# A decoder layer on one core: one more pair by seven products in five groups, and the memory mixed block by block

## The chip, the cores and the metric

The kernel runs on one core of a Trainium2 chip. Its time is the time of one execution on the device in microseconds (us), as a median of several runs. The engines named below are TensorE (PE in the rows; it multiplies matrices, and its weight loads are PEld), VectorE (DVE), ScalarE (ACT), GpSimd (POOL) and SyncE (SP, which issues nearly all DMAs). Matrix products accumulate in PSUM banks of 128 x 512 numbers; everything else lies in SBUF.

## What is computed

One layer of a decoder for 256 tokens of width 2048, in f32: a token mixer (mLSTM heads and dilated attention heads behind one input projection), cross-attention into 256 memory tokens, and a SwiGLU channel mixer, each with a residual and a layer norm. Cut to what carries the weights:

```python
def reference(x, mem, w_in, gate_b, conv_w, conv_b, mh_g, rel_bias, w_out, xq, xk, xv, xo,
              w1, w3, w2, ln_g, ln_b):
    for l in range(DEPTH):
        proj = x @ w_in[l]
        q_m, k_m, v_m, o_m, i_m, f_m, q_a, k_a, v_a = split_columns(proj, IN_SPLITS)
        y_m = mlstm_mixer(q_m, k_m, v_m, o_m, i_m, f_m, conv_w[l], conv_b[l], gate_b[l], mh_g[l])
        y_a = dilated_attention(q_a, k_a, v_a, rel_bias)
        y = jnp.concatenate([y_m, y_a], axis=-1) @ w_out[l]
        x = layer_norm(DEEPNORM_ALPHA * x + y, ln_g[l, 0], ln_b[l, 0])
        y = memory_cross_attention(x, mem, xq[l], xk[l], xv[l], xo[l])
        x = layer_norm(DEEPNORM_ALPHA * x + y, ln_g[l, 1], ln_b[l, 1])
        y = swiglu_ffn(x, w1[l], w3[l], w2[l])
        x = layer_norm(DEEPNORM_ALPHA * x + y, ln_g[l, 2], ln_b[l, 2])
    return x
```

`memory_cross_attention` computes `x @ wq`, `mem @ wk`, `mem @ wv`, a softmax over the memory tokens and `o @ wo`; `swiglu_ffn` is `(silu(x @ w1) * (x @ w3)) @ w2` with a hidden width of 5632.

## The kernel before

**Precision.** A matmul takes its operands in a reduced f32 format. So `split` (L112 to L115) writes each operand as a high part, a cast on ScalarE (L114), and a low part, the rest, by a subtraction on VectorE (L115). A product of two split operands takes three matmuls: high by high, high by low, low by high. Tokens and memory are split once (`Operand.put`); the weights, 1 MB at a time, are split as they arrive.

**Groups and pairs.** Each weight product is cut into groups of 1024 output columns. A group is the sum over 2048 input rows in eight pairs (w2, over a half of the hidden width, in twelve): a pair is two tiles of 128 input rows by 1024 columns, one DMA (L199, or L210 where two arrays are read) into one of three raw buffers (RAW). Split weights have five buffers for each part (SPLIT).

**A plain pair** takes 24 matmuls of 128x512 (two token halves, two row tiles, two column halves, three each). **A pair by seven products** treats the pair as a 2 x 2 block matrix times a 2 x 2 block matrix and uses seven block products in place of eight: 21 matmuls. For this VectorE forms sums of the weight blocks (`sums`: L292 over 1024 columns, L296 and L297 over 512), which are split as well, and the token block has to be mixed (`Operand.mix`: four differences of 128x128, L145 to L148, and a split of 512 columns). Where the unsplit token block is gone, `mix_again` first adds high and low part (L156). In `gemm_seven` a plan gives the order of pairs: a number is a plain pair, a number in brackets, as `(2,)`, is a pair by seven products. The products go to eight PSUM banks: P1, P5, P7 and Q6 belong to sevens alone; once the last seven of the plan is through, `early` (L652 to L669 or L671 to L686) combines them, and P2, P3, Q4 and E are added at the end of the group (L691 in `whole`, L650 in `add`).

**Order of the stages on TensorE**, with the names that the rows carry: input features i0 and i1, first rows v0, attention with i2 and i3, gates, i4 and i5, v1, v2, i6, i7 and the mLSTM, memory keys xk0 and xk1, output projection wo0 and wo1, xk2 and xk3, memory values xv0 and xv1, queries xq0 to xq3 with the cross-attention, its output xo0 and xo1, then the channel mixer: f0 to f10 (the first half of the hidden units), w2a0 and w2a1 (the second product's first half, one group for each half of the columns), f12 to f20, w2b0 and w2b1, and the last norm.

**Order within an engine.** Each engine takes its instructions strictly in the order of its queue. That order is fixed when the kernel is built, by a scheduler that reorders the program on a modelled timeline; so an edit in one place moves rows in others. `tc.issue_after(latest["lo"])` puts the instructions under it behind the latest low part. Small tiles come from a pool of NSLOT slots of 4 KB for each partition (`big` takes a slot, `slot` half of one); a slot is used again as soon as its last reader is through, and the next writer waits for that reader.

**Mixing.** The blocks of x are mixed ahead of v0 (`in_rows`), the blocks of the memory ahead of xv0 (VALUES = 1, 4, 6), those of the attention's output ahead of xo0. `hidden` turns the hidden units of each f group by TensorE transposes into `hT`; the blocks in SEVENS are copied out of PSUM (L1123) and mixed at once, the others only split. hT in rows is a high or low part of such a block, hTm a mixed one.

Of the kernel before, what the change touches and what calls it, by code (L numbers as in the profile page):

```python
# [11 lines left out]
F32 = mybir.dt.float32  # L12
# [7 lines left out]
P = 128  # L20
# [14 lines left out]
W = 1024  # L35
NSLOT, RAW, SPLIT = 34, 3, 5
LAG, HEAD, POOLED, LAG2 = 6, 8, 5, 8
WARM = 2

SEVENS = (2, 4, 6, 8, 13, 15, 17)  # L40

# [11 lines left out]
def decoder_layer(ctx: ExitStack, tc: tile.TileContext, A):  # L53
# [726 lines left out]
    def in_rows(i):  # L780
        rows, plan = [], [0, 1, (2,), 3, 4, (5,), 6, 7]
        if not xT.mixed:
            xT.mix_again(2)
            xT.mix_again(5)
        banks = gemm_seven(xT, fetch(A["w_v"][i], f"v{i}"), KT, f"v{i}", plan, into_rows(rows, f"v{i}r"))
        whole(rows, banks)
        return rows
# [10 lines left out]
    nc.sync.dma_start(out=gb, in_=A["gate_b"])  # L798
    gw = const.tile([P, KT, 8], F32, tag="gw", name="gw")
    nc.sync.dma_start(out=gw, in_=A["w_gate"])  # L800

    gw2 = const.tile([P, KT, 40], F32R, tag="gw2", name="gw2")
    gz = slot("gwz")
# [10 lines left out]
    es, least_norm = gates()  # L814
    free(sel_t)
    for j in range(2):
# [77 lines left out]
    vx, x1 = [[None] * 4 for _ in range(2)], Operand("x1")  # L894
    with tc.issue_after(latest["lo"]):
        for j in VALUES:
            memT.mix_again(j)

# [14 lines left out]
    one, two, three = VALUES  # L913
    values(0, [0, 2, (one,), 3, (two,), 5, (three,), 7])
    values(1, [(one,), 0, (two,), 2, (three,), 3, 5, 7], turn_in)
# [66 lines left out]
    ln = Norm(1, "l1")  # L982
    for j in (1, 3):
        oT.mix_again(j)
    plan = [0, 2, (1,), 4, (3,), 5, 6, 7]
    banks = gemm_seven(oT, fetch(A["xo"][0], "xo0"), KT, "xo0", plan, into_z(0, ALPHA))
# [147 lines left out]
    def w2_first():  # L1134
        plan = [0, 1, 3, (2,), 5, (4,), 7, (6,), 9, (8,), 10, 11]
        for c in range(2):
            banks = gemm_seven(
                hT, fetch(A["w2"][c][:half], f"w2a{c}"), 2 * half, f"w2a{c}", plan, into_z(c, ALPHA),
                last=c == 1,
            )  # L1140
            for m in range(2):
                add(m, c, banks, scale=1.0)
# [129 lines left out]
```

## Time and profile before

| | |
|---|---|
| median of 3 runs | 1541.11 us (1541.36, 1539.5, 1541.11) |
| the profiled execution's own time | 1540.81 us |
| its span, first to last instruction | 1539.0 us, so 1.8 us lie around it |
| mean granted TensorE clock | 0.998 |
| busy: VectorE, ScalarE, GpSimd | 1233.4, 797.0, 9.3 us |
| moved by DMA | 301.37 MB, 196 GB/s over the span |

In the rows below, a line of the timeline gives start, duration, engine, line of the kernel, operation and tile; in brackets stands how long the engine idled just before, and what ended that. Buffer numbers are left out there, so that `xv0l` is any low part of xv0's weights, and `xk3r` any slot that was first called so. A row with x2 or more joins instructions that follow each other on that engine. The rows of busy time in stretches give for each stretch its length, then the busy us of PE, PEld, DVE, ACT and POOL with the count of instructions, the granted clock, the busy share of the DMA engines and GB/s.

### The profile page before, as it was taken

How to read it: one execution, taken by the hardware profiler on the slowest of the kernel's cores; microseconds unless marked ns; L12 is line 12 of the kernel's file. 1: busy time of each engine (PE TensorE's matmuls, PEld its weight loads, DVE VectorE, ACT ScalarE, POOL GpSimd, SP SyncE). 2: the span in 40 equal slices, each digit the busy share in tenths (PEclk: the TensorE clock that was granted, in tenths of full speed). 3: DMA queues.
4: the chain of work that ended last, by engine and by line, in shares of the span. 5: the costliest groups of instructions: out<-in, count | busy, mean ns of one | idle time of the engine just before them, and what ended most of it. 6: DMA issues, size and time to landing. Idle time of an engine off the chain costs nothing.

```text
span 1539.0 us, 19369 instructions
## 1 busy us (share of the span) xinstructions
PE 1522.7 (99%) x7394; PEld 1273.8 (83%) x7394; DVE 1233.4 (80%) x1663; ACT 797.0 (52%) x1054; POOL 9.3 (1%) x18
## 2 busy tenths in 40 slices
PE   9999999999999999999999999999999999999997
PEld 7888888888888878888888888887788888888885
DVE  7665788787799888657798788888788878888897
ACT  5444645554544555445557454555545455455551
POOL 0000000000000000000000000000000000000000
PEclk9999999999999999999999999999999999999999
DMA  8674445664654546445564555665455666567552
GB/s 303 208 272 165 140 172 210 232 237 160 232 191 172 205 171 221 162 165 179 177 218 165 174 182 192 218 195 200 156 215 208 200 192 194 192 205 260 197 186 109
DMA packets 83419, 301.37 MB, mean 196 GB/s; under 512 B 7213, under 2 KB 9466, under 8 KB 59774
## 3 DMA queue, kind: packets, MB, share of 16 engines
q1 hardware_dynamic: 83326, 300.14, 56.6%
q8 instruction: 58, 0.95, 0.2%
q14 instruction: 35, 0.29, 0.1%
HBM read 297.99 MB, written 4.21 MB: 196 GB/s over the span
## 4 chain that ended last, share of the span: by engine, by line
PE 95%; DVE 3%; DMA 1%; issue 0%; ACT 0%; DVEq 0%; SPq 0%; ACTq 0%
PE w2a1P L323 2%; PE w2a0P L323 2%; PE w2b0P L323 2%; PE w2b1P L323 2%; PE f10P L323 2%; PE v1P L323 2%; PE xo0P L323 2%; PE wo0P L323 2%; PE f4P L323 2%; PE f14P L323 2%; PE f6P L323 2%; PE f20P L323 2%; PE f16P L323 2%; PE f18P L323 2%; PE v0P L323 2%; PE wo1P L323 2%
## 5 line engine op out<-in xcount | busy, mean ns | idle before, releaser
L114 ACT CAST w2a1h<-w2a1w 128x1024 fp32r<-128x1024 f32 (+1 forms) x24 | 22.5, 980 | 23.3 <-PE w2a1E L323 14.5
L114 ACT CAST w2a0h<-w2a0w 128x1024 fp32r<-128x1024 f32 (+1 forms) x24 | 22.8, 980 | 17.8 <-PE w2a0E L323 10.7
L115 DVE TENSOR_TENSOR w2a0l<-w2a0w,w2a0h 128x1024 fp32r<-128x1024 f32 (+1 forms) x24 | 26.5, 1129 | 6.1 <-ACT w2a0h L114 6.1
L115 DVE TENSOR_TENSOR w2a1l<-w2a1w,w2a1h 128x1024 fp32r<-128x1024 f32 (+1 forms) x24 | 26.3, 1128 | 5.6 <-ACT w2a1h L114 5.6
L114 ACT CAST w2b0h<-w2b0w 128x1024 fp32r<-128x1024 f32 (+1 forms) x20 | 19.3, 987 | 17.3 <-PE w2b0E L323 9.8
L114 ACT CAST w2b1h<-w2b1w 128x512 fp32r<-128x512 f32 (+1 forms) x28 | 19.8, 758 | 12.9 <-PE w2b0E L323 5.4
L323 PE MATMUL w2a0P<-w2a0h,hT 128*128 128x512 f32 x80 | 26.2, 391 | 0.2 <-ACT w2a0h L114 0.2
L323 PE MATMUL w2a1P<-w2a1h,hT 128*128 128x512 f32 x80 | 25.4, 389 | 0.0
L114 ACT CAST wo1h<-wo1w 128x1024 fp32r<-128x1024 f32 (+1 forms) x16 | 15.6, 1001 | 18.9 <-PE wo1E L323 11.3
L264 PE MATMUL f0b<-f0h,x 128*128 128x512 f32 x64 | 25.4, 397 | 0.0
L114 ACT CAST f12h<-f12w 128x1024 fp32r<-128x1024 f32 (+1 forms) x16 | 15.6, 1000 | 18.7 <-PE f12E L323 9.9
L265 PE MATMUL f0b<-f0l,x 128*128 128x512 f32 x64 | 25.1, 392 | 0.1
L114 ACT CAST xv0h<-xv0w 128x1024 fp32r<-128x1024 f32 (+1 forms) x16 | 15.2, 970 | 18.5 <-PE xv0E L323 7.1
L115 DVE TENSOR_TENSOR w2b0l<-w2b0w,w2b0h 128x1024 fp32r<-128x1024 f32 (+1 forms) x20 | 22.2, 1137 | 3.0 <-ACT w2b0h L114 3.0
L115 DVE TENSOR_TENSOR v0l<-v0w,v0h 128x1024 fp32r<-128x1024 f32 (+1 forms) x16 | 18.2, 1154 | 7.8 <-ACT v0h L114 7.7
L115 DVE TENSOR_TENSOR xo0l<-xo0w,xo0h 128x1024 fp32r<-128x1024 f32 (+1 forms) x16 | 18.2, 1153 | 7.3 <-ACT xo0h L114 7.2
L114 ACT CAST v0h<-v0w 128x1024 fp32r<-128x1024 f32 (+1 forms) x16 | 15.7, 1000 | 16.0 <-PE v0E L323 9.9
L114 ACT CAST v2h<-v2w 128x1024 fp32r<-128x1024 f32 (+1 forms) x16 | 15.6, 1000 | 16.2 <-PE v2E L323 10.8
L115 DVE TENSOR_TENSOR w2b1l<-w2b1w,w2b1h 128x512 fp32r<-128x512 f32 (+1 forms) x28 | 22.7, 854 | 1.5 <-ACT w2b1h L114 1.5
L387 PE MATMUL i0b<-xT,i0h 128*128 128x512 f32 x64 | 22.6, 427 | 0.8 <-ACT i0h L114 0.8
L115 DVE TENSOR_TENSOR wo0l<-wo0w,wo0h 128x1024 fp32r<-128x1024 f32 (+1 forms) x16 | 18.2, 1153 | 6.4 <-ACT wo0h L114 6.4
L387 PE MATMUL xk1b<-mT,xk1h 128*128 128x512 f32 x64 | 23.0, 401 | 0.3 <-ACT xk1h L114 0.3
(1719 smaller groups left out, 5556.6 us busy)
## 6 DMA issues: line engine op xcount, KB each, us to landing
w2a0w<-in_w SPq DMA_DIRECT2D x12, 1024.0 KB, 4.8
w2a1w<-in_w SPq DMA_DIRECT2D x12, 1024.0 KB, 5.7
w2b0w<-in_w SPq DMA_DIRECT2D x10, 1024.0 KB, 4.9
w2b1w<-in_w SPq DMA_DIRECT2D x10, 1024.0 KB, 5.0
v0w<-in_w_v SPq DMA_DIRECT2D x8, 1024.0 KB, 5.1
v1w<-in_w_v SPq DMA_DIRECT2D x8, 1024.0 KB, 4.8
v2w<-in_w_v SPq DMA_DIRECT2D x8, 1024.0 KB, 4.8
wo0w<-in_w_out SPq DMA_DIRECT2D x8, 1024.0 KB, 4.9
```

Of the source, the lines that this page charges most:

```text
L114: SC.copy(hi, src)
L115: latest["lo"] = V.tensor_tensor(out=lo, in0=src, in1=as_f32(hi), op=ALU.subtract).ins
L264: T.matmul(banks[m][c], xh, wh[:, cs], start=n == 0, stop=False)
L265: T.matmul(banks[m][c], xh, wl[:, cs], start=False, stop=False)
L323: T.matmul(of[to], lhsT, rhs, start=to not in begun, stop=end)
L387: T.matmul(banks[f], wh[:, cs], op.both(kt), start=kt == 0, stop=end, skip_group_check=True)
```

## The change

Five groups (v0, v2, xo0, w2a0, w2a1) take one more pair by seven products and one plain pair less. v1 keeps two sevens, with block 4 in place of block 5. For this, block 4 and 6 of x in place of block 5, block 5 of the attention's output and block 10 of the hidden units are mixed as well. In w2a's plan the sevens now stand at every second place from the third on. The memory's blocks are mixed one after each pair of xv0's plan (`mix_next`), no longer all three ahead of it. There is one slot more; the gates' two weight tiles move from a pool of their own into slots that are freed behind the gates.

```diff
--- before.py
+++ after.py
@@ -33,11 +33,11 @@
 NEG = -1.0e30
 U = 2 * S - 1
 W = 1024
-NSLOT, RAW, SPLIT = 34, 3, 5
+NSLOT, RAW, SPLIT = 35, 3, 5
 LAG, HEAD, POOLED, LAG2 = 6, 8, 5, 8
 WARM = 2
 
-SEVENS = (2, 4, 6, 8, 13, 15, 17)
+SEVENS = (2, 4, 6, 8, 10, 13, 15, 17)
 
 VALUES = (1, 4, 6)
 
@@ -778,10 +778,10 @@
         return features(gemm_features(xT, A["w_qk"][i], f"i{i}", load, last), f"i{i}")
 
     def in_rows(i):
-        rows, plan = [], [0, 1, (2,), 3, 4, (5,), 6, 7]
+        rows, plan = [], [0, 1, (2,), 3, (4,), 5, *([6] if i == 1 else [(6,)]), 7]
         if not xT.mixed:
-            xT.mix_again(2)
-            xT.mix_again(5)
+            for j in (2, 4, 6):
+                xT.mix_again(j)
         banks = gemm_seven(xT, fetch(A["w_v"][i], f"v{i}"), KT, f"v{i}", plan, into_rows(rows, f"v{i}r"))
         whole(rows, banks)
         return rows
@@ -796,10 +796,11 @@
     nc.sync.dma_start(out=cw, in_=A["conv"])
     gb = const.tile([8, 1], F32, tag="gb", name="gb")
     nc.sync.dma_start(out=gb, in_=A["gate_b"])
-    gw = const.tile([P, KT, 8], F32, tag="gw", name="gw")
+    gw_t, gw2_t = slot("gw"), big("gw2")
+    gw = gw_t[:, : KT * 8].rearrange("p (k c) -> p k c", k=KT)
     nc.sync.dma_start(out=gw, in_=A["w_gate"])
 
-    gw2 = const.tile([P, KT, 40], F32R, tag="gw2", name="gw2")
+    gw2 = gw2_t[:, : KT * 40].rearrange("p (k c) -> p k c", k=KT)
     gz = slot("gwz")
     V.memset(gz, 0.0)
     V.tensor_copy(gw2[:, :, 8:32], gz.rearrange("p (k c) -> p k c", k=KT)[:, :, :24])
@@ -812,7 +813,7 @@
         attention(2 * j, qk0[j], qk0[2 + j], [va[m][0] for m in range(2)], tb)
     qk1 = in_features(2) + in_features(3)
     es, least_norm = gates()
-    free(sel_t)
+    free(sel_t, gw_t, gw2_t)
     for j in range(2):
         attention(4 + 2 * j, qk1[j], qk1[2 + j], [va[m][1] for m in range(2)], tb)
     free(*va[0], *va[1])
@@ -892,9 +893,12 @@
 
 
     vx, x1 = [[None] * 4 for _ in range(2)], Operand("x1")
-    with tc.issue_after(latest["lo"]):
-        for j in VALUES:
-            memT.mix_again(j)
+    to_mix = list(VALUES)
+
+    def mix_next():
+        if to_mix:
+            with tc.issue_after(latest["lo"]):
+                memT.mix_again(to_mix.pop(0))
 
     def values(g, plan, between=None):
         rows = []
@@ -911,7 +915,7 @@
             x1.put(j, turned([z[m][j // 2] for m in range(2)], j % 2, f"x1p{j}"))
 
     one, two, three = VALUES
-    values(0, [0, 2, (one,), 3, (two,), 5, (three,), 7])
+    values(0, [0, 2, (one,), 3, (two,), 5, (three,), 7], mix_next)
     values(1, [(one,), 0, (two,), 2, (three,), 3, 5, 7], turn_in)
 
 
@@ -980,9 +984,9 @@
         cross(h)
 
     ln = Norm(1, "l1")
-    for j in (1, 3):
+    for j in (1, 3, 5):
         oT.mix_again(j)
-    plan = [0, 2, (1,), 4, (3,), 5, 6, 7]
+    plan = [0, 2, (1,), 4, (3,), 6, (5,), 7]
     banks = gemm_seven(oT, fetch(A["xo"][0], "xo0"), KT, "xo0", plan, into_z(0, ALPHA))
     for m in range(2):
         ln.add(m, 0, banks, scale=1.0)
@@ -1132,7 +1136,7 @@
     n, half = FFN // 256, 12
 
     def w2_first():
-        plan = [0, 1, 3, (2,), 5, (4,), 7, (6,), 9, (8,), 10, 11]
+        plan = [0, 1, (2,), 3, (4,), 5, (6,), 7, (8,), 9, (10,), 11]
         for c in range(2):
             banks = gemm_seven(
                 hT, fetch(A["w2"][c][:half], f"w2a{c}"), 2 * half, f"w2a{c}", plan, into_z(c, ALPHA),
```

Three places show what moves on VectorE. The first is the begin of xv0, the first half of the memory values (mT is the memory, mTr and the slot xk3r hold blocks that are being mixed, mTm a mixed block, xv0t and xv0s the sums for a seven). Before:

```order
L115 TENSOR_TENSOR kx6_4583<-xk2r1_4386,kx6_4583 128x2x256
L296 TENSOR_TENSOR xv0s1_4729<-xv0t1_4728,xv0w1_4726 128x512
L115 TENSOR_TENSOR kx7_4586<-xk3t0_4573,kx7_4586 128x2x256
L156 TENSOR_TENSOR xk3r1_4578<-mT1_3122 128x512
L156 TENSOR_TENSOR mTr1_4623<-mT4_3222 128x512
L156 TENSOR_TENSOR mTr4_4632<-mT6_3274 128x512
L297 TENSOR_TENSOR xv0s1_4729<-xv0s1_4729,xv0w1_4726 128x512
L292 TENSOR_TENSOR xv0t4_4806<-xv0w4_4804 128x1024
L145 TENSOR_TENSOR xk3r1_4578<-xk3r1_4578 128x128
L146 TENSOR_TENSOR xk3r1_4578<-xk3r1_4578 128x128
L145 TENSOR_TENSOR mTr1_4623<-mTr1_4623 128x128
L146 TENSOR_TENSOR mTr1_4623<-mTr1_4623 128x128
```

Changed:

```order
L115 TENSOR_TENSOR xv0l1_4674<-xv0w0_4655,xv0h1_4673 128x1024
L156 TENSOR_TENSOR xk3r1_4602<-mT1_3146 128x512
L145 TENSOR_TENSOR xk3r1_4602<-xk3r1_4602 128x128
L146 TENSOR_TENSOR xk3r1_4602<-xk3r1_4602 128x128
L292 TENSOR_TENSOR xv0t1_4743<-xv0w1_4741 128x1024
L147 TENSOR_TENSOR xk3r1_4602<-xk3r1_4602 128x128
L115 TENSOR_TENSOR xv0l4_4701<-xv0w2_4698,xv0h4_4700 128x1024
L296 TENSOR_TENSOR xv0s1_4744<-xv0t1_4743,xv0w1_4741 128x512
L148 TENSOR_TENSOR xk3r1_4602<-xk3r1_4602 128x128
L115 TENSOR_TENSOR xv0l5_4717<-xv0w2_4698,xv0h5_4716 128x1024
L156 TENSOR_TENSOR mTr1_4689<-mT4_3246 128x512
L403 TENSOR_TENSOR xk2r1_4410<-xk3b0_4421,xk2r1_4410 128x256
```

Before, the three additions L156 stood together behind xv0s1's first sum (L296), and the mixing of the three blocks went on interleaved. Now block 1 is mixed first, alone, among the low parts of the two plain pairs, and block 4 (read out of mT4) begins some nine rows later.

The second place is the group f10 while the hidden units of f8 are turned and mixed (f8ru becomes the mixed block hTm8; f10t2 and f10s2 are the sums for the seven of pair 2). Before:

```order
L145 TENSOR_TENSOR f8ru_8875<-f8r11_8878 128x128
L146 TENSOR_TENSOR f8ru_8875<-f8r11_8878 128x128
L147 TENSOR_TENSOR f8ru_8875<-f8r11_8878,f8ru_8875 128x128
L115 TENSOR_TENSOR hT9_8988<-f8p1_8983,hT9_8988 128x2x256
L148 TENSOR_TENSOR f8ru_8875<-f8r11_8878,f8ru_8875 128x128
L115 TENSOR_TENSOR f10l2_9095<-f10t2_9072,f10h2_9094 128x1024
L115 TENSOR_TENSOR hT8_8969<-f8r11_8878,hT8_8969 128x2x256
L115 TENSOR_TENSOR hTm8_8976<-f8ru_8875,hTm8_8976 128x512
L296 TENSOR_TENSOR f10s2_9073<-f10t2_9072,f10w2_9069 128x512
L297 TENSOR_TENSOR f10s2_9073<-f10s2_9073,f10w2_9069 128x512
L115 TENSOR_TENSOR f10l2_9105<-f10s2_9073,f10h2_9104 128x1024
```

Changed:

```order
L292 TENSOR_TENSOR f10t2_9115<-f10w2_9112 128x1024
L296 TENSOR_TENSOR f10s2_9116<-f10t2_9115,f10w2_9112 128x512
L691 TENSOR_TENSOR f8ru_8918<-f8ru_8918,f8P2_8680 128x512
L115 TENSOR_TENSOR f10l3_9097<-f10w1_9077,f10h3_9096 128x1024
L691 TENSOR_TENSOR f8r00_8919<-f8r00_8919,f8P3_8681 128x512
L297 TENSOR_TENSOR f10s2_9116<-f10s2_9116,f10w2_9112 128x512
L691 TENSOR_TENSOR f8r00_8919<-f8r00_8919,f8Q4_8682 128x512
L691 TENSOR_TENSOR f8r01_8920<-f8r01_8920,f8E_8683 128x512
```

The sums of f10s2 (L296, L297) stood behind the mixing of block 8 and its two subtractions; now they stand ahead of the mixing, among the additions that end f8.

The third place is the begin of w2a0 while the hidden units of f10 are turned (w2a0t2 and w2a0s2 are the sums for its first seven, w2a0t4 and w2a0s4 for its second). Before:

```order
L115 TENSOR_TENSOR w2a0l2_9462<-w2a0w2_9447,w2a0h2_9461 128x1024
L292 TENSOR_TENSOR w2a0t2_9449<-w2a0w2_9447 128x1024
L292 TENSOR_TENSOR w2a0t4_9527<-w2a0w4_9525 128x1024
L115 TENSOR_TENSOR hT11_9334<-f10p1_9329,hT11_9334 128x2x256
L296 TENSOR_TENSOR w2a0s2_9450<-w2a0t2_9449,w2a0w2_9447 128x512
L115 TENSOR_TENSOR w2a0l2_9472<-w2a0t2_9449,w2a0h2_9471 128x1024
L297 TENSOR_TENSOR w2a0s2_9450<-w2a0s2_9450,w2a0w2_9447 128x512
L296 TENSOR_TENSOR w2a0s4_9528<-w2a0t4_9527,w2a0w4_9525 128x512
L297 TENSOR_TENSOR w2a0s4_9528<-w2a0s4_9528,w2a0w4_9525 128x512
L115 TENSOR_TENSOR w2a0l2_9482<-w2a0s2_9450,w2a0h2_9481 128x1024
```

Changed:

```order
L292 TENSOR_TENSOR w2a0t2_9466<-w2a0w2_9464 128x1024
L145 TENSOR_TENSOR f10ru_9272<-f10r11_9275 128x128
L146 TENSOR_TENSOR f10ru_9272<-f10r11_9275 128x128
L115 TENSOR_TENSOR hT10_9366<-f10r11_9275,hT10_9366 128x2x256
L297 TENSOR_TENSOR w2a0s4_9545<-w2a0s4_9545,w2a0w4_9542 128x512
L147 TENSOR_TENSOR f10ru_9272<-f10r11_9275,f10ru_9272 128x128
L115 TENSOR_TENSOR w2a0l2_9489<-w2a0t2_9466,w2a0h2_9488 128x1024
L148 TENSOR_TENSOR f10ru_9272<-f10r11_9275,f10ru_9272 128x128
L115 TENSOR_TENSOR hTm10_9373<-f10ru_9272,hTm10_9373 128x512
L115 TENSOR_TENSOR hT11_9385<-f10p1_9380,hT11_9385 128x2x256
L296 TENSOR_TENSOR w2a0s2_9467<-w2a0t2_9466,w2a0w2_9464 128x512
L297 TENSOR_TENSOR w2a0s2_9467<-w2a0s2_9467,w2a0w2_9464 128x512
```

Before, w2a0s2's sums stood behind the two subtractions that end hT10 and hT11. Now the mixing of block 10 (L145 to L148 and hTm10) stands ahead of them too, between w2a0t2 and w2a0s2, and the seven that needs w2a0s2 comes one plain pair earlier in the plan.

## Prediction

> **What bounds the kernel now.** I read the page first: how busy each engine is, then by engine the chain that ended last.
>
> ```profile
> PE 1522.7 (99%) x7394; PEld 1273.8 (83%) x7394; DVE 1233.4 (80%) x1663; ACT 797.0 (52%) x1054; POOL 9.3 (1%) x18
> PE 95%; DVE 3%; DMA 1%; issue 0%; ACT 0%; DVEq 0%; SPq 0%; ACTq 0%
> ```
>
> TensorE is the bound: 95% of the chain is matmuls, and only some 16 us of 1539 are not covered by one. A matmul less is time less, unless TensorE then waits. Pieces of the same chain in order of time (start, length) give the price of a matmul:
>
> ```profile
> 863.21 4.76 PE f2P L323 x21
> 1035.58 5.44 PE f10P L323 x24
> 1079.83 5.44 PE w2a0P L323 x24
> ```
>
> 5.44 / 24 = 0.2267 us for a 128x512 matmul, so a plain pair takes 5.44 us and a pair by seven products 21 x 0.2267 = 4.76 us. The list of what TensorE waited for shows where it stands still at all (total us, times, longest), and the timeline shows single waits:
>
> ```profile
> PE w2a0Q L323 <- ACT w2a0h L114: 0.5, 1, 0.5
> PE xv0P L323 <- DVE xv0l L115: 0.5, 2, 0.3
> PE xv1P L323 <- DVE mTr L691: 0.5, 1, 0.5
> PE xv0P L323 <- ACT mTm L114: 0.5, 1, 0.5
> PE f10Q L323 <- ACT f10h L114: 0.3, 1, 0.3
> PE xv1P L323 <- DVE xv0ru L691: 0.3, 1, 0.3
> PE w2a0P L323 <- ACT w2a0h L114: 0.2, 1, 0.2
> PE f10P L323 <- ACT f10h L114: 0.2, 1, 0.2
> ...
> 1100.55 0.40 PE L323 MATMUL w2a0P<-w2a0h,hTm 128*128 128x512 f32 x1
> 1101.48 0.50 PE L323 MATMUL w2a0Q<-w2a0h,hTm 128*128 128x512 f32 x1 [0.54 <-ACT w2a0h L114]
> ```
>
> The matmul at 1101.48 begins 0.93 us after the one ahead of it, where 0.23 is usual. So a wait costs 0.70 where the list shows 0.54: about 0.17 more than its idle time. Counted so, xv0's three waits cost 1.0 + 3 x 0.17 = 1.5 us, xv1's two 1.15, f10's two 0.9, w2a0's two 1.05. Busy time by stretch says how near the other engines are (length; busy PE, PEld, DVE, ACT):
>
> ```profile
> 53.00:96.00 43.00, 43.00 (x189) 34.65 (x187) 27.52 (x32) 18.47 (x21) 0.00 (x0) 1.00 0.74 257
> 525.50:569.40 43.90, 42.88 (x186) 34.11 (x185) 39.36 (x57) 24.08 (x29) 0.00 (x0) 1.00 0.49 170
> 722.00:773.00 51.00, 51.00 (x261) 43.55 (x261) 39.31 (x52) 24.80 (x33) 0.00 (x0) 1.00 0.57 196
> 1079.60:1145.00 65.40, 64.54 (x287) 52.39 (x286) 54.25 (x63) 33.44 (x38) 0.00 (x0) 1.00 0.54 193
> 1145.00:1207.50 62.50, 62.50 (x277) 51.76 (x276) 51.42 (x56) 31.36 (x33) 0.00 (x0) 1.00 0.59 202
> 1476.00:1528.00 52.00, 52.00 (x231) 43.08 (x230) 46.62 (x66) 22.71 (x31) 0.91 (x1) 1.00 0.40 142
> ```
>
> v0 (first row) has 15 us of free VectorE, w2a0 and w2a1 (fourth and fifth) some 11. w2b1 (last) runs VectorE at 46.62 / 52.00 = 90% and TensorE never waits there, so a full VectorE alone is no stall.
>
> **Matmuls removed.** Five plain pairs become sevens: 5 x 3 x 0.2267 = **-3.4 us**, all on the chain.
>
> **VectorE work added.** Prices from start to start, out of xv0:
>
> ```profile
> 535.03 0.68 DVE L296 TENSOR_TENSOR xv0s<-xv0t,xv0w 128x512 f32<-128x512 f32 x1
> 535.63 0.28 DVE L147 TENSOR_TENSOR xk3r<-xk3r 128x128 f32<-128x128 f32 x1
> 535.84 0.48 DVE L147 TENSOR_TENSOR mTr<-mTr 128x128 f32<-128x128 f32 x2
> 536.24 1.22 DVE L115 TENSOR_TENSOR xv0l<-xv0t,xv0h 128x1024 fp32r<-128x1024 f32 x1
> 537.38 1.22 DVE L115 TENSOR_TENSOR xv0l<-xv0s,xv0h 128x1024 fp32r<-128x1024 f32 x1
> 538.51 0.68 DVE L297 TENSOR_TENSOR xv0s<-xv0s,xv0w 128x512 f32<-128x512 f32 x1
> ```
>
> A 128x1024 step takes 1.14 us, 128x512 0.60, 128x128 0.20. A converted pair adds L292 (1.14), L296 and L297 (1.20) and 1.5 wide subtractions (1.71): 4.05 us. A block mixed again adds L156, four small ones and a subtraction, 2.0 us; hT10, which needs no L156, 1.4, and on ScalarE a copy. Together 5 x 4.05 + 2 x 2.0 + 1.4 = 26 us in 42 instructions. The cover: in v0 (and v2, alike) 15 us free against 4.05; in xo0 51.00 - 39.31 = 11.7 against 6.1; in w2a1 11 against 4.05; in w2a0 11 against 5.5. I cost this at 0 but for the place in w2a0 below. Were the cover gone, each us over it would be a us of the time. The gates' tiles in slots and the one slot more I cost at 0: loaded tens of us ahead of the gates, as before; bounds -0.3 to +0.3, a wait like the shortest ones in the list either way.
>
> **Memory mixed block by block.** Before, xv0's first sevens stood behind three blocks' mixing, 3 x 2.0 us of VectorE, of which the first seven needs one. In the changed order block 1 is mixed among the low parts of the plain pairs, so what xv0P waited for (mTm) is there some 4 us earlier. What is late next is xv0l of the second seven, which has only its own mixing ahead of it; VectorE idled in between before:
>
> ```profile
> 547.05 1.23 DVE L292 TENSOR_TENSOR xv0t<-xv0w 128x1024 f32<-128x1024 f32 x1 [3.17 <-DMA xv0w<-in_xv]
> 572.07 0.50 PE L323 MATMUL xv1P<-xv1h,mT 128*128 128x512 f32 x1 [0.51 <-DVE mTr L691]
> ```
>
> Into those 3.17 us the work pushed back by the two later blocks (4 us) nearly fits. xv1's waits are for additions L691 that free banks, on a VectorE that was running behind; with 3 us caught up they should come in time, by about 0.5 us as I follow the rows. I take xv0 and xv1 as freed: 1.5 + 1.15 = **-2.65**. Bounds: all of it, or nothing.
>
> **f10.** Its wait was for the high part of f10s:
>
> ```profile
> 1050.06 1.05 ACT L114 CAST f10h<-f10s 128x1024 fp32r<-128x1024 f32 x1 [2.85 <-DVE f10s L297]
> 1051.17 0.50 PE L323 MATMUL f10Q<-f10h,x2m 128*128 128x512 f32 x1 [0.34 <-ACT f10h L114]
> 1052.11 0.73 PE L323 MATMUL f10P<-f10h,x 128*128 128x512 f32 x2 [0.21 <-ACT f10h L114]
> ```
>
> In the changed order both sums stand ahead of the mixing of block 8, some 9 us earlier, so the wait goes: **-0.9** (0 to -0.9). Late next would be hTm8, which nothing needs before w2a.
>
> **w2a0.** Here the change builds the order that f10 loses: the mixing of block 10 stands ahead of w2a0s2's sums. f10 is the nearest measure. Its cast ended at 1050.06 + 1.05 = 1051.11, which is 15.53 us after f10's start (1035.58); TensorE came to it at 1051.17 - 0.50 = 1050.67, 15.09 after. On w2a0's start (1079.83) that is a cast ending at 1095.36 and TensorE there at 1094.92, since the seven now stands third. But w2a0t2 (1.14) and w2a0s4's L297 (0.60) also stand between the transposes and the sums, so the cast ends at 1097.1: a wait of 2.2, and with the high parts queued behind it on ScalarE (the next two of 128x1024, needed within two matmuls), about 0.5 more. 2.7 + 2 x 0.17 = 3.0 against the 1.05 paid today: **+2.0**. Bounds: 0.9 as in f10 (net -0.1), or 3.8 if every step of VectorE's queue from the last transpose on is laid end to end (+2.75).
>
> **Ends of groups and queues.** In w2a0 and w2a1 the last seven moves to the place before the last, so the eight additions after it (L657 to L666) run just ahead of the four L650 that free the banks for the next group. Before, TensorE did not wait at either place; some 0.60 us steps are pushed late. Between 0 and three steps (1.8), I take **+0.5**. v0 ends 0.7 us sooner, but i2's weights do not come sooner: their DMAs stand on SP behind the bias table's.
>
> ```profile
> 93.45 2.00 ACT L114 CAST i2h<-i2w 128x1024 fp32r<-128x1024 f32 x2 [7.98 <-DMA i2w<-in_w_qk]
> ```
>
> ScalarE waited for them already. Between 0 and 0.7, I take **+0.3**.
>
> **Sum.** -3.4 - 2.65 - 0.9 + 2.0 + 0.5 + 0.3 = -4.15. From the profiled execution's 1540.81 us (span 1539.0 and 1.8 around it) that is 1536.7. The median of the three runs, 1541.11, lies 0.3 above the profiled one. 0.2%, about what a measurement of this kernel can tell from no change, is 3.1 us: faster means below 1538.0, slower above 1544.2.
>
> **A rule that would change w2a0's price.** A clock that starts slow is seen at the begin:
>
> ```profile
> 8.79 1.91 PE L387 MATMUL i0b<-xT,i0h 128*128 128x512 f32 x4
> 10.49 0.78 PE L388 MATMUL i0b<-xT,i0l 128*128 128x256 f32 x4
> ```
>
> Four 128x512 matmuls there take 10.49 - 8.79 = 1.70, or 0.425 each, against 0.2267 later. The Trainium skill, "TensorE: Matmul & The Clock Gate", "Part 1: The HAM clock gate", says that such a half clock comes back once TensorE has been idle for a window of about 3.4 us, and lasts about as long. No run here has yet shown a second slow stretch. As a mechanism of this kernel: a wait in w2a0 in one piece as long as my upper bound, then eight matmuls at 0.425 in place of 0.2267, 8 x 0.2 = +1.6.
>
> **Rivals.**
> (a) *The mixing only shifts.* xv0 and xv1 keep their 2.65 at other rows, since VectorE has the same work there (39.36 of 43.90). For it: xv1's waits are for banks, not for mixing. Against: the 3.17 us of idle VectorE. -3.4 - 0.9 + 2.0 + 0.8 = -1.5: 1539.3. Chance 0.22.
> (b) *Lock-step in w2a.* With sevens at every second place, VectorE waits for high parts, those for split buffers, those for TensorE; if it has to idle as long as now (65.40 - 54.25 = 11.15 and 62.50 - 51.42 = 11.1 us), the groups are bound by it: w2a0 54.25 + 5.45 + 11.15 = 70.85, w2a1 51.42 + 4.05 + 11.1 = 66.6, against 64.7 and 61.8 after the removal: +6.1 and +4.8. With the other terms -3.4 - 2.65 - 0.9 + 0.3 + 10.9 = +4.3: 1545.1, slower. It decides once VectorE idles over 64.7 - 59.7 = 5 us in w2a0. Against: w2b1 at 90%, three sevens in ten pairs, without a wait. Chance 0.10.
> (c) *The half clock after w2a0's wait:* 1536.7 + 0.8 + 1.6 = 1539.1. The trace bears out only the price: 0.03.
> (d) *w2a0's wait stays as f10's was:* -2.1 on the forecast, 1534.6. Chance 0.15.
> (e) *It doesn't do what it says,* if TensorE is not held by matmuls where they go: the 43.00 of 43.00 busy in v0 speaks against it. Time unchanged but for moved rows, 1540.8. Chance 0.05.
>
> **Numbers.** The forecast itself has 0.45: 1536.7 us. With (d) and a few near 1538.0 from (a): faster 0.62. Same, from (a), (c), (e) and the weak half of (b): 0.28. Slower 0.10. The range runs from 1533.0 (all stalls gone and w2a0 as f10) to 1541.5 (rival (a) with w2a0 and the ends of the groups at their upper bounds, 1539.3 + 0.75 + 1.3); what (b) gives above is left out.
>
> **What would show it.** 15 matmuls of 128x512 fewer and groups v0, v2, xo0 shorter by 0.68 each; no rows for xv0P, xv1P and f10Q in the list of waits; a wait of w2a0Q for ScalarE's w2a0h of 2 us or more. A new row of over 1 us in w2a1 or f12, or VectorE idle above 5 us in w2a0 with TensorE idle too, would make the prediction wrong.

## The result and the profile after

The changed kernel is **slower**: 1557.45 us as the median of 4 runs (1555.53 to 1561.39), against 1540.86 for the kernel before (4 runs). The ratio is 1.0112, with an interval of 1.0092 to 1.0133, so 16.6 us are lost where 4 were forecast as gained. The profiled execution took 1561.39 us (span 1559.6), 20.6 us more than the profiled one of before.

The page of the changed kernel, busy time by engine and the chain by engine:

```profile
PE 1525.7 (98%) x7379; PEld 1272.4 (82%) x7379; DVE 1261.4 (81%) x1705; ACT 806.2 (52%) x1068; POOL 11.4 (1%) x18
PE 90%; DVE 4%; DMA 4%; ACT 1%; issue 1%; SPq 1%; DVEq 0%; ACTq 0%
```

TensorE has 15 matmuls less (7394 to 7379), yet its share of the chain fell from 95% to 90%: 90% of 1559.6 us leaves about 156 us in which the chain runs through something else, where 5% of 1539.0 were 77. VectorE got 42 instructions and 28.0 us more, close to the 26 forecast. So the work came out as reckoned; the loss is in waiting: TensorE stands idle 1559.6 - 1525.7 = 33.9 us where it was 16.3. (Its busy time rose by 3.0 us all the same; a part of the reason is given at the end.) What TensorE waited for (total us, times, longest):

```profile
PE w2a0Q L323 <- ACT w2a0h L114: 3.4, 1, 3.4
PE pt L497 <- DVE xTr L493: 2.5, 1, 2.5
PE pt L497 <- DVE g L493: 2.4, 1, 2.4
PE i2b L387 <- ACT i2h L114: 1.6, 1, 1.6
...
PE i2b L388 <- DVE i2l L115: 1.3, 1, 1.3
PE xk1b L387 <- DVE xk0t L403: 1.2, 1, 1.2
...
PE xo1P L323 <- ACT xo1h L114: 1.2, 1, 1.2
```

The waits of xv0P, xv1P and f10Q are gone, as forecast, and w2a0Q's is there. But most of the others are in the mixer (L497 turns the weights of attention; i2b is its third group of input features), in the memory keys (xk1b) and in xo1. Of these the prediction priced only i2's weights, at +0.3.

To place the loss, I took the start of the first matmul of a stage in both traces. The difference after - before grows by these amounts over each stretch (worked out from the timelines; us):

```
start to v0             +1.5
v0 to i3                +3.0    (v0 and i2)
i3 to v2               +13.3    (attention, i4, i5, gates, v1)
v2 to wo0               +1.3
wo0 to xv0              -0.3
xv0 to the queries      -4.0
queries, attention, xo  +3.6    (to the first matmul of f0)
f0 to f10                0.0
f10 to w2a0             -1.2
w2a0 to f14             +3.8
f14 to w2b1's end       -0.5
sum                    +20.6    (of the unrounded rows)
```

These are single traces. Kernels of this document that are alike up to wo0 differ there by up to 1.5 us, most of it between v0 and i3, so a smaller difference is not read in that stretch.

More than half of the loss lies in attention, where the change touches nothing but where two small tiles live.

**A wait in attention.** TensorE's timeline in the changed kernel, at head 3 (sc holds scores, pt the turned weights):

```profile
138.58 0.38 PE L480 MATMUL sc<-i0r 128*128 128x128 f32 x2
138.72 0.36 PE L388 MATMUL i3b<-xT,i3l 128*128 128x256 f32 x1
138.92 0.40 PE L387 MATMUL i3b<-xT,i3h 128*128 128x512 f32 x1
139.16 0.28 PE L388 MATMUL i3b<-xT,i3l 128*128 128x256 f32 x1
141.96 0.30 PE L497 MATMUL pt<-ident,xTr 128*128 128x128 f32 x1 [2.52 <-DVE xTr L493]
```

And VectorE's, for the softmax between:

```profile
139.00 0.56 DVE L482 SCALAR_TENSOR_TENSOR xTr<-sc,tb 128x384 f32<-128x384 f32 x1 [7.74 <-PE sc L480]
...
141.27 0.55 DVE L493 TENSOR_SCALAR xTr<-xTr,ast 128x256 f32<-128x256 f32 x2
```

The softmax of a head takes 141.27 + 0.55 - 139.00 = 2.8 us, and here nothing is in its way: VectorE had been idle 7.74 us before it and starts at once. TensorE needs 2.8 / 0.2267 = 12.4, so 13 matmuls of 128x512, of other work between a head's scores (L480) and its transposes (L497). Here it has three, two of them half as wide. Counted in the traces, as 128x512 matmuls between the two, heads 0 to 7, in this and two later kernels:

```
before                        39    32    27    42.5  34    55    41.5  64
changed                       40.5  28.5  31     2    42     9     1.5  46
gates' tiles in slots alone   39    32    34.5   2    42     9     1.5  46
change with another slot      44.5  30    32.5  43    34    55    41.5  48
```

Three heads of the changed kernel are not covered: 3, 5 and 6. TensorE waits 2.5, 0.9 and 2.4 us at them, 5.9 in all, and 1.4 us in two smaller waits behind head 6; matmuls at half clock behind head 3 cost 1.8 us more (see the end). The rest of the 13.3 us is not taken apart. What the other engines waited for in 85 to 225 us points to why the order is another. Changed kernel:

```profile
DVE v0r L403 <- PE po L503: 5.7, 1, 5.7
...
DVE me L403 <- PE po L503: 2.1, 1, 2.1
...
ACT g L402 <- PE pt L497: 1.3, 1, 1.3
...
```

L402 and L403 copy the results of i2 and i4 out of PSUM into slots. In the changed kernel they are handed slots that a head still holds, so the copies wait for that head's transposes (L497) and products (L503); before, one such row of 2.1 us stands in the same stretch. The matmuls of the input features, which cover the softmax, need those banks. The order is built with the gates' matmuls drawn up: the first of them (L514) stands behind 673 matmuls in the trace, where it stood behind 748, and too few are left for the later heads. That the waiting copies are what drew them up is argued, not shown: in the change with another slot one copy (L402) waits 3.5 us for L497, and no head lacks cover.

### The profile page after: what moved, and what is told of

Its sections match the earlier page's. It is cut to its first block, busy times and chain, and to the rows that moved or that the text cites. A ratio compares the mean times of both kernels' runs of the same rounds, so it can differ in the third digit from the quotient of the medians.

```text
span 1559.6 us, 19404 instructions
## 1 busy us (share of the span) xinstructions
PE 1525.7 (98%) x7379; PEld 1272.4 (82%) x7379; DVE 1261.4 (81%) x1705; ACT 806.2 (52%) x1068; POOL 11.4 (1%) x18
## 4 chain that ended last, share of the span: by engine, by line
PE 90%; DVE 4%; DMA 4%; ACT 1%; issue 1%; SPq 1%; DVEq 0%; ACTq 0%
PE w2a1P L323 2%; PE w2a0P L323 2%; PE w2b0P L323 2%; PE w2b1P L323 2%; PE xv1P L323 2%; PE xv0P L323 2%; PE v2P L323 2%; PE f6P L323 1%; PE f4P L323 1%; PE wo0P L323 1%; PE f14P L323 1%; PE f16P L323 1%; PE f18P L323 1%; PE f20P L323 1%; PE wo1P L323 1%; PE f10P L323 1%
## 5 line engine op out<-in xcount | busy, mean ns | idle before, releaser
L114 ACT CAST w2b1h<-w2b1w 128x512 fp32r<-128x512 f32 (+1 forms) x28 | 19.8, 759 | 12.4 <-PE w2b0E L323 5.4
L387 PE MATMUL i2b<-xT,i2h 128*128 128x512 f32 x64 | 23.0, 399 | 1.6 <-ACT i2h L114 1.6
L114 ACT CAST f20h<-f20w 128x1024 fp32r<-128x1024 f32 (+1 forms) x16 | 15.8, 999 | 15.3 <-PE f20E L323 7.2
L323 PE MATMUL w2b0P<-w2b0h,hT 128*128 128x512 f32 x68 | 23.0, 391 | 0.0
L387 PE MATMUL xq2b<-x,xq2h 128*128 128x512 f32 x64 | 23.0, 399 | 0.0
```

What stands on the lines that cost most here:

```text
L114: SC.copy(hi, src)
L323: T.matmul(of[to], lhsT, rhs, start=to not in begun, stop=end)
L387: T.matmul(banks[f], wh[:, cs], op.both(kt), start=kt == 0, stop=end, skip_group_check=True)
```

## The experiments

Two theories were set against each other at first, beside a third, that the loss is in w2a0 and xo1. *Slots:* the loss in the mixer is the gates' tiles in slots, since a slot more or less taken changes every hand-out behind it. *Sevens:* it is the new sevens and mixings of v0, v1 and v2 on VectorE. All ratios below are against the kernel before on the same chip, with a 95% interval.

### The gates' tiles in slots, alone

```diff
-NSLOT, RAW, SPLIT = 34, 3, 5
+NSLOT, RAW, SPLIT = 35, 3, 5
-    gw = const.tile([P, KT, 8], F32, tag="gw", name="gw")
+    gw_t, gw2_t = slot("gw"), big("gw2")
+    gw = gw_t[:, : KT * 8].rearrange("p (k c) -> p k c", k=KT)
...
-    free(sel_t)
+    free(sel_t, gw_t, gw2_t)
```

> Only the gates' two weight tiles go into slots, with one slot more; no matmul is removed. Theory S (slots): the shifted hand-out of slots makes the results of i2 and i4 wait for attention's last reads, so that TensorE has 2, 9 and 1 matmuls (before: 43, 55 and 41) between three heads' scores and their transposes. Then most of the change's loss is here: 10 to 14 us slower than before, with rows for pt waiting on L493 in TensorE's list of waits. Theory M (the mixer's added VectorE work and its third seven): no more than 1 us from before. Theory L (the loss is in w2a0 and xo1): no more than 1 us from before.

1547.52 against 1541.04 us: 1.0045 (1.003 to 1.006), 6.5 us lost with no matmul changed. Up to wo0 it loses 12.0 us of the whole change's 19.1, at the same heads (its first gate matmul stands behind 676); the waits are as long at heads 3 and 6, and 1.8 us against 0.9 at head 5. Then it gains some back, since the hand-out differs there as well (xv0 and xv1 -3.9, f10 -1.2, w2a -1.7). The expected size was missed for that reason; the mechanism stands:

```profile
DVE v0r L403 <- PE po L503: 4.1, 1, 4.1
...
DVE me L403 <- PE po L503: 2.1, 1, 2.1
```

```profile
137.31 0.30 PE L497 MATMUL pt<-ident,xTr 128*128 128x128 f32 x1 [2.52 <-DVE xTr L493]
```

The first fence is the waits in 85 to 225 us, the second TensorE's timeline: head 3 again, and again 2.52 us.

### The whole change, with the slot taken from the other end

The narrow tile stays in its own pool; the wide one takes the slot that would be handed out last, and gives it back ahead of the second norm.

```diff
-    gw_t, gw2_t = slot("gw"), big("gw2")
-    gw = gw_t[:, : KT * 8].rearrange("p (k c) -> p k c", k=KT)
+    gw = const.tile([P, KT, 8], F32, tag="gw", name="gw")
+    gi = free_slots.pop()
+    gw2_t = up.tile([P, 1024], F32R, tag=f"u{gi}", name="gw2")
+    held[id(gw2_t)] = (gi, gw2_t)
...
-    free(sel_t, gw_t, gw2_t)
+    free(sel_t)
...
+    free(gw2_t)
     ln = Norm(1, "l1")
```

> The whole change, but gw2 takes the added slot from the end of the list and keeps it until the cross-attention is through, and gw stays in its own pool; all other tiles are handed out as before. Theory S: 11 to 15 us faster than the changed kernel's 1557.5, so 1543 to 1546: -3.4 for matmuls, -4 in xv, -1.2 in f10, +4.3 in w2a0, +3.4 in xo1, +4 in i1, v0 and i2. Theory M: stays at 1556 to 1558. Theory L: stays within 2 us of 1557.5.

1549.86 us: 1.0056 (1.0041 to 1.0071). With every seven and every mixing of the change in place, 7.6 us of the 16.6 are gone, no head lacks cover (last row of the counts), and the first gate matmul stands behind 741 again. The other 9 us are not the slots of attention: this kernel is 5.5 us behind at wo0, gains 3.5 in xv0 and xv1, loses 6.6 between the queries and f0, and 2.4 in w2a. Neither theory alone holds; that is why it came out above the expected range.

### The new sevens of the mixer, alone

```diff
-        rows, plan = [], [0, 1, (2,), 3, 4, (5,), 6, 7]
+        rows, plan = [], [0, 1, (2,), 3, (4,), 5, *([6] if i == 1 else [(6,)]), 7]
         if not xT.mixed:
-            xT.mix_again(2)
-            xT.mix_again(5)
+            for j in (2, 4, 6):
+                xT.mix_again(j)
```

> Only the plans of v0, v1 and v2 and the third mixed block of x. Theory S: -1.4 for six matmuls, +1.5 in i1 and +3 between v0 and i2 as in the changed kernel's trace, so 2 to 4 us slower than before, and no long wait in attention. Theory M: 10 to 15 us slower. Theory L: 1 us faster.

1544.68 us: 1.0025 (1.0016 to 1.0035), 3.6 us lost with six matmuls fewer. The trace puts it at two places: +3.5 us from v0 to i3, and +1.9 from v1 to v2. The first is i2's weights. SyncE's issues before:

```profile
62.45 0.33 SPq L199 DMA_DIRECT2D v0w<-in_w_v  x1
...
86.37 10.88 SPq L247 DMA_DIRECT2D i2w<-in_w_qk  x4
```

In this experiment:

```profile
63.79 0.33 SPq L199 DMA_DIRECT2D v0w<-in_w_v  x1
...
88.03 11.12 SPq L247 DMA_DIRECT2D i2w<-in_w_qk  x4
```

v0's sixth pair is read 1.34 us later, when its raw buffer comes free. The bias table stands behind it on SyncE, and i2's weights behind that, 1.66 us later than before. ScalarE was already waiting for them, and TensorE waits 1.7 and 1.3 us, much as in the changed kernel. But the late issue is not enough: in the next experiment i2's weights are issued just as late (87.99 us), and TensorE does not wait. What differs is the built order:

```profile
96.46 0.50 PE L387 MATMUL i2b<-xT,i2h 128*128 128x512 f32 x1 [1.72 <-ACT i2h L114]
96.80 0.62 PE L323 MATMUL v0P<-v0l,xT 128*128 128x512 f32 x2
```

The first matmul of i2 stands ahead of the last eight of v0, and those, 8 x 0.2267 = 1.8 us of work, stand behind its wait of 1.72. It is so in all three kernels with v0's third seven and in no other kernel here. The second wait, for a low part of i2, is not taken apart.

### Both mixer groups, apart

Here v0 has two sevens, as before, but at pairs 2 and 4; v1 has the changed plan, and v2 the third seven. Blocks 2, 4 and 6 are mixed as in the change.

```diff
-        rows, plan = [], [0, 1, (2,), 3, 4, (5,), 6, 7]
+        rows, plan = [], [0, 1, (2,), 3, (4,), 5, *([(6,)] if i == 2 else [6]), 7]
```

> As the run with the mixer's sevens alone, but v0 has two sevens, (2) and (4), and only v2 has a third. If the loss of 3.6 us comes from v0's third seven by way of i2's weights: no wait of i2b over 0.5 us, and 0 to 1 us faster than before. If it comes from the third mixed block or the moved plans: 2 to 4 us slower, as with all.

1542.26 us: 1.001 (1.0001 to 1.0019), 1.7 lost. i3 starts 0.8 us late where it was 3.8, and i2's waits are gone, so v0's third seven costs 2 to 3 us (1.9 by the two medians, 3.0 by the starts of i3). But v1 to v2 still loses 1.9:

```profile
PE v1Q L323 <- ACT v1h L114: 0.7, 1, 0.7
```

v1 keeps two sevens; its second only stands at pair 4 and not 5. That costs the 1.9, and v2's third seven gains 0.8. The time lies in neither of the two ranges expected. By the spacing of the matmuls 1.6 of the 1.9 us lie at that wait and two shorter ones beside it, from 230.8 to 233.4 us. The high part comes late because of VectorE's sum for that seven:

```profile
229.38 0.69 DVE L296 TENSOR_TENSOR v1s<-v1t,v1w 128x512 f32<-128x512 f32 x1 [1.94 <-PE po L504]
```

The sum reads nothing of attention, but VectorE stands idle until a product of a head (L504) is through, as it would where the sum is handed that head's slot. The same row stands in the experiment before this one and in the last one below; in the kernel before, no sum of v1 waits for L504. So the place costs by way of a slot again, as far as the profile tells.

### The memory mixed block by block, alone

```diff
-    with tc.issue_after(latest["lo"]):
-        for j in VALUES:
-            memT.mix_again(j)
+    to_mix = list(VALUES)
+
+    def mix_next():
+        if to_mix:
+            with tc.issue_after(latest["lo"]):
+                memT.mix_again(to_mix.pop(0))
...
-    values(0, [0, 2, (one,), 3, (two,), 5, (three,), 7])
+    values(0, [0, 2, (one,), 3, (two,), 5, (three,), 7], mix_next)
```

> Only the memory mixed block by block. All three theories: xv0 and xv1 lose their waits, 2.5 to 4.5 us faster than before. If the gain in xv comes from later reorderings instead, 0 to 1 us faster.

1538.59 us: 0.9985 (0.9976 to 0.9995), a gain of 2.45, just short of the range expected. All of it is xv0's (-2.3 to xv1's start); xv1's wait for a bank stays:

```profile
PE xv1P L323 <- DVE mTr L691: 1.1, 1, 1.1
```

### xo0's third seven, late and early

Late, as in the change, the seven stands last but one; early, a plain pair more stands behind it.

```diff
-    for j in (1, 3):
+    for j in (1, 3, 5):
         oT.mix_again(j)
-    plan = [0, 2, (1,), 4, (3,), 5, 6, 7]
+    plan = [0, 2, (1,), 4, (3,), 6, (5,), 7]      late
+    plan = [0, 2, (1,), 4, (3,), (5,), 6, 7]      early
```

> Only xo0's third seven, as in the change (plan 0 2 (1) 4 (3) 6 (5) 7). Theory E (ends of groups): with a seven in the place before the last, the eight additions of the early part, the four that free the banks and xo1's first seven meet on VectorE; xo1 takes 4 to 6 us more, so 3 to 5 us slower than before. Theory S (all loss is the slots'): 0.7 us faster.

> As the run before it, but block 5 comes right behind block 3, with two plain pairs behind it (plan 0 2 (1) 4 (3) (5) 6 7). Theory E: the eight additions fall into the two plain pairs, xo1 is as long as before, and the stage is 0.7 us shorter: 0 to 1 us faster than before, or up to 2 slower if two sevens in a row run VectorE late. If the loss comes from the third seven wherever it stands, as slow as the late one.

Late: 1545.41 against 1540.48 us, 1.0028 (1.0018 to 1.0039), 4.9 lost. Early: 1542.18, 1.0012 (1.0003 to 1.0022), 1.7 lost, so the place makes up 3.2 of it. VectorE's timeline of the late one, at the seam from xo0 to xo1:

```profile
779.27 1.21 DVE L292 TENSOR_TENSOR xo1t<-xo1w 128x1024 f32<-128x1024 f32 x1
780.39 0.68 DVE L663 TENSOR_TENSOR oTr<-oTr,xo0P 128x512 f32<-128x512 f32 x1
780.99 0.68 DVE L665 TENSOR_TENSOR oTr<-oTr,xo0P 128x512 f32<-128x512 f32 x1
781.59 0.68 DVE L650 SCALAR_TENSOR_TENSOR xk1r<-xk1r,xo0P 128x512 f32<-128x512 f32 x1
782.18 1.22 DVE L115 TENSOR_TENSOR xo1l<-xo1s,xo1h 128x1024 fp32r<-128x1024 f32 x1
...
787.46 0.68 DVE L650 SCALAR_TENSOR_TENSOR z<-z,xo0E 128x512 f32<-128x512 f32 x1
```

Each row starts where the one before ends, without a bracket, from 771 to 792 us: VectorE is full there, although xo0 as a whole had 11.7 us free. Before, it was already without a gap from 771.7 to 788.8 us; now it has none from 768.8 to 803.9. The eight additions L657 to L666 that end a seven, and the four L650 that free the banks, run into xo1's own sums, and TensorE waits twice (same kernel, timeline):

```profile
781.20 0.73 PE L323 MATMUL xo1P<-xo1h,oT 128*128 128x512 f32 x2 [1.20 <-ACT xo1h L114]
...
788.19 0.50 PE L323 MATMUL xo1E<-xo1h,oT 128*128 128x512 f32 x1 [0.66 <-DVE z L650]
```

The second wait is for an L650. The first is for a high part, and ScalarE had itself stood idle 4.15 us until a matmul of xo1 was through, so that one is not shown to be VectorE's. What is shown is the price of the place, 3.2 us. Of what the early one still loses, 1.2 us are two waits in the cross-attention (0.7 and 0.2 us), which the late one has too.

### w2a's plan: as changed; early without block 10; with a spare slot

As changed, w2a has five sevens from the third place on, block 10 is mixed, and the slot comes from the other end. The second experiment takes the early places alone, with four sevens, no block 10 and no slot more. The third adds a slot to that, which the group's first sum gets.

```diff
-        plan = [0, 1, 3, (2,), 5, (4,), 7, (6,), 9, (8,), 10, 11]
+        plan = [0, 1, (2,), 3, (4,), 5, (6,), 7, (8,), 9, (10,), 11]      as changed
+        plan = [0, 1, (2,), 3, (4,), 5, (6,), 7, (8,), 9, 10, 11]         early, both others
...
+        held.pop(id(gw2_t))                                               spare slot
+        free_slots.insert(0, gi)
```

> Only the plan of w2a and the mixing of block 10, with gw2 in the added last slot. From the changed kernel's trace: w2a0 is 2.5 to 4.5 us longer by a wait of 3.4 at w2a0Q, f10 1.2 shorter if its order comes from this edit, w2a1 0.7 shorter: 0 to 3 us slower than before. Theory S: 1.4 us faster.

> Only w2a's first four sevens moved one plain pair forward, pairs 9, 10 and 11 plain: no matmul removed, and block 10 not mixed. If w2a0's wait comes from the mixing of block 10 ahead of the first seven's sums, the wait at w2a0Q is 1 to 2 us and the time is within 1.5 us of before. If it comes from the first seven standing one plain pair earlier, the wait is 3 us or more: 2 to 5 us slower.

> As the run with w2a's sevens one pair forward and block 10 not mixed, but the first wide sum of w2a0 (w2a0t2) gets a slot that was kept free for it, so it no longer waits for f10's transposes. If the wait in w2a0 comes from the slot that the sum shares with f10's hidden units, the waits at w2a0P of 2.3 and 1.5 us go, and the time is 2 to 4 us less than that run's 1545.3: 1541 to 1543. If it comes from VectorE having too much work there, the waits stay and the time is within 1 us of 1545.3.

As changed: 1543.07 against 1540.48, 1.0019 (1.001 to 1.0028), 2.6 lost. By the starts of the stages 3.2 of it lie in w2a (w2a0 to f14), and f10 is 1.2 shorter. (This trace is also 1.2 longer in the mixer. That is not the slot's: the run with the spare slot and the one of the parts that gain have the same slot taken and VectorE's order unchanged there, and are 0.3 and 0.0 longer.) Early without block 10: 1545.34, 1.0029 (1.0017 to 1.0041), 4.9 lost, so the early places are enough for a loss. Its waits:

```profile
PE w2a0P L323 <- ACT w2a0h L114: 2.3, 1, 2.3
PE w2a0P L323 <- DVE w2a0l L115: 1.5, 1, 1.5
```

What its tile w2a0t, the first sum, waited for (releaser, total us, times):

```profile
  PE f10p L1118: 3.5, 1
```

The sum is handed a slot that f10's hidden units hold until TensorE's transposes (L1118) have read them. In the kernel before it stands idle 2.64 us for them as well, but there the seven comes a plain pair later. With the spare slot the kernel takes 1542.2 against 1540.69, 1.001 (1.0001 to 1.0019), and both waits are gone. Another shows in their place:

```profile
PE w2a0Q L323 <- ACT w2a0h L114: 2.2, 1, 2.2
```

A slot is behind this one too. VectorE's next sum for the seven (w2a0s) now stands idle for the same transposes, here L1121:

```profile
1093.46 1.29 DVE L296 TENSOR_TENSOR w2a0s<-w2a0t,w2a0w 128x512 f32<-128x512 f32 x2 [2.24 <-PE f10p L1121]
```

So in the early order without block 10 the sums are late because f10 still holds their slots, and the early place brings TensorE there before them. The two are not separated here. In the runs below each of them alone, a later place or other slots, takes away even the short waits that w2a0 had before.

### The parts that gain, together

From these runs: the memory block by block; w2a's five sevens, but with four plain pairs ahead of the first and pairs (4,) and (6,) side by side; the slot from the other end; the mixer and xo0 as before.

```diff
-        plan = [0, 1, 3, (2,), 5, (4,), 7, (6,), 9, (8,), 10, 11]
+        plan = [0, 1, 3, 5, (2,), 7, (4,), (6,), 9, (8,), (10,), 11]
```

> Memory block by block, and w2a with its five sevens, the first of them only behind four plain pairs (plan 0 1 3 5 (2) 7 (4) (6) 9 (8) (10) 11), gw2 in the added last slot until the cross-attention. If w2a0's wait comes from sums that are late against a fixed moment, four plain pairs cover it: memory -2.4, f10 -1.2, six matmuls -1.4, w2a0's wait -1 to -2: 1534 to 1536. If sevens that stand together run VectorE late, w2a0 and w2a1 give 2 to 4 us back: 1537 to 1540.

1534.92 against 1540.69 us: 0.9965 (0.9952 to 0.9977). It beats both kernels. What TensorE waited for:

```profile
PE pw L430 <- POOL idle L428: 1.5, 1, 1.5
PE f12Q L323 <- DVE z L650: 1.0, 1, 1.0
...
```

No wait is left in xv0, xv1, f10 or w2a0. Two runs on the same chip split it: the memory with the slot and no plan changed, and the memory with later places in w2a, no seven and no slot more:

```diff
-        plan = [0, 1, 3, (2,), 5, (4,), 7, (6,), 9, (8,), 10, 11]
+        plan = [0, 1, 3, 5, (2,), 7, (4,), 9, (6,), (8,), 10, 11]
```

> Memory block by block, and gw2 in the added last slot until the cross-attention; no plan changed. If f10's gain comes from slots handed out in another order (its sums stand ahead of the mixing here too), it is there without any change of w2a: memory -2.4, f10 -1.2, w2a0 0 to -1.5: 1536 to 1537.5. If f10's gain needs the mixing of block 10, only the memory's: 1538.6.

> Memory block by block, and w2a's four sevens one plain pair later (plan 0 1 3 5 (2) 7 (4) 9 (6) (8) 10 11), no slot added, no matmul removed in w2a. If w2a0's wait comes from sums late against a fixed moment: -2.4 and -1 to -2 in w2a0: 1536.5 to 1537.5. If not: 1538.6 or more.

1535.99 us, 0.9969 (0.9958 to 0.9979), and 1536.91 us, 0.9975 (0.9965 to 0.9985). By the starts of the stages the slot takes 1.2 us off f10 and 1.6 off w2a0 with no plan touched; the later places take 1.7 off w2a0 with no slot. Last, the best with v2's third seven and the changed places in v0 and v1:

```diff
-        rows, plan = [], [0, 1, (2,), 3, 4, (5,), 6, 7]
+        rows, plan = [], [0, 1, (2,), 3, (4,), 5, *([(6,)] if i == 2 else [6]), 7]
```

> The fastest kernel so far (memory block by block, w2a with five late sevens) with v2's third seven, v0 at two. If v0's third seven was the cause: 0.7 us less than that kernel, 1533.5 to 1535. If the third mixed block costs: 1537 to 1539.

1535.87 against 1540.56 us, 0.9968 (0.9956 to 0.9981): not to be told from the kernel without it. By the starts of the stages v1's places lose 1.9 us and v2's seven saves 0.6. Neither expectation names this.

## Why the prediction was wrong

**The step that failed** is one sentence: "The gates' tiles in slots and the one slot more I cost at 0 ... bounds -0.3 to +0.3". It went by when the two tiles are loaded and read. Their cost is elsewhere: every tile behind them gets another slot, and in attention copies wait for slots that a head still holds, and three softmaxes lose their cover. Alone the step costs 6.5 us, and undoing it in the whole change gives 7.6 back. No rival covered it. The order was shown at three places, where the diff edits a plan; attention was not among them.

Term by term:

- **Matmuls removed, -3.4:** right in count, 15 rows fewer; v2's third seven, where the cover held, gained 0.8 us in the run with v0 and v1 apart.
- **VectorE's work at 0 by cover:** wrong in kind. The cover was an average over a stage (15 us free in v0, 11.7 in xo0). In xo0 the work came at the seam, where VectorE was full, and cost 4.9 alone, 3.2 of it by its place. I priced "ends of groups" at +0.5 and named only w2a, where the changed kernel has no wait in w2a1 or f12.
- **i2's weights, +0.3 (0 to 0.7):** the queue was right, its size not. With the sevens alone v0's sixth pair is read 1.34 us later, and behind it i2's weights are issued 1.66 us later. But a delay like that alone made no wait. What I left out is that TensorE's order moves as well: i2's first matmul now stands ahead of v0's last eight. With v0's third seven this is 2 to 3 us.
- **v1's second seven one pair earlier:** no term for it; 1.9 us.
- **Memory, -2.65:** 2.45 measured alone, all in xv0; -4.0 over xv0 and xv1 in the whole. Rival (a), that the mixing only shifts, is out for xv0. In xv1 the wait for a bank stays in three of the four kernels that take the memory's edit without the mixer's (1.1, 0.9 and 1.2 us) and goes in the fourth, the one of the parts that gain; why there is open.
- **f10, -0.9:** -1.2 measured, and the mechanism was right. Before, the mixing of f8's block begins 9.4 us after f10's first matmul and the sums of f10's first seven 13.2 after; in the changed kernel these sums begin 0.3 us ahead of it and the mixing 11.5 after. What brings this order is the slot: it is the same in the run with the gates' tiles alone and in the one with the memory and the slot, where no plan of w2a is edited.
- **w2a0, +2.0:** right in kind; the wait was 3.45 us, 3.6 as a cost, between the 3.0 taken and the upper bound of 3.8. The chain of the changed kernel shows the queue that was forecast, the sums behind the mixing and the subtractions:

```profile
1111.16 0.21 DVE f10ru L148
...
1111.39 0.63 ACT hTm L114
...
1112.05 0.69 DVE hTm L115
1112.74 0.60 DVE hT L115
1113.34 0.61 DVE w2a0s L296
...
1113.97 0.70 DVE w2a0s L297
...
1114.76 1.05 ACT w2a0h L114
...
1115.85 1.22 PE w2a0Q L323 x2
```

The early place is needed for it, as forecast: with four plain pairs ahead of the first seven, and block 10 mixed as well, no wait is left. How much of the 3.45 us the mixing alone makes was not measured.

- **The half clock, rival (c):** it came true at w2a0, and at a place that I had not named. Windows of the changed kernel behind the waits (stretch, length, busy PE, PEld, DVE, ACT, POOL, granted clock, DMA share, GB/s):

```profile
142.30:146.00 3.70, 3.70 (x21) 2.75 (x20) 0.00 (x0) 1.03 (x3) 0.00 (x0) 0.54 0.00 0
1115.60:1122.00 6.40, 6.15 (x14) 4.64 (x15) 5.96 (x6) 4.61 (x6) 0.00 (x0) 0.50 0.69 233
```

After each wait the granted clock is about half. By the spacing of the matmuls (0.427 where 0.227 is usual at 128x512) this costs 3.1 us over 14 matmuls in w2a0, 1.5 more than the +1.6 put down for it, and 1.8 us over 18 narrow matmuls behind head 3. That is a part of why TensorE's busy time rose with 15 matmuls less.

Rival (b), lock-step in w2a, did not happen: w2a0 lost one wait and one stretch of half clock, no steady drag. The parts measured alone, 6.5 + 3.6 - 2.45 + 4.9 + 2.6 = 15.2, come near the whole's 16.6. That they add up so well is partly luck: a slot is in two of them, each edit shifts slots of its own, and some of these runs contain a half clock as well.

What stays open: by what step another hand-out of slots becomes another order in attention, why v0's third seven draws i2's first matmul up, and whether the 1.2 us that the cross-attention loses in both of xo0's runs come from the slot that block 5's mixing takes.

## What to carry to other kernels

Where tiles are handed out of one list in turn, a tile that is added or freed elsewhere changes which buffer every later tile gets; so compare the whole built order with that of before, and count the cover behind each fixed latency (here 13 matmuls for a softmax), not only at the edited lines. Cover has to be read at the few microseconds where the new work lands, above all at the seam of two groups, and never as the idle time of a stage. After an edit that makes a stage shorter or its loads later, look whether the built order has put a waiting matmul of the next stage ahead of the last ones of this stage.

## What was not expected of the hardware

The half clock came after a wait of 2.52 us at head 3, and lasted 3.4 us (142.5 to 145.9). In the run with the gates' tiles alone the same wait of 2.52 us left the clock whole:

```profile
137.30:141.30 4.00, 3.99 (x33) 3.56 (x34) 0.02 (x1) 1.03 (x3) 0.00 (x0) 1.00 0.00 0
```

There it fell behind head 6, after a wait of 2.43 us and one of 0.6, and again for 3.4 us:

```profile
201.00:204.40 3.40, 3.40 (x13) 2.93 (x12) 3.16 (x9) 0.40 (x1) 0.00 (x0) 0.50 0.00 0
```

In the changed kernel the same wait of 2.43 us at head 6 left it at 1.00. So of two kernels with the same two waits, each lost the clock behind another one.

The Trainium skill, "TensorE: Matmul & The Clock Gate", "Part 1: The HAM clock gate", gives about 3.4 us as the idle window after which the clock halves, and calls the window free-running. The wait in w2a0 (3.45 us) agrees, and so do those of 3.44 and 3.42 us at the same place in the change with another slot and in w2a as changed: each was followed by a clock of 0.50. The ones of 2.52 and 2.43 us do not agree with the length. That the window is free-running may have to do with why the same wait halved the clock once and not the other time, but no run here shows the window itself. Behind w2a0's shorter waits in the early order without block 10 (2.3 and 1.5 us, two matmuls between them) the granted clock was 0.50 as well, for 6.8 us, and some twelve matmuls ran at half clock. The half clock may be part of why the changed kernel's runs spread over 1555.53 to 1561.39 where those of before lie within 1.9 us: the fastest has a mean granted clock of 0.996, the other three 0.994. That was not tried.
